# Sliding-window attention with its two heads side by side, and a position bias that a skewed transfer shapes instead of a product

## The chip, the cores and the metric

The kernel runs on one core of one Trainium2 chip. The metric is the device time of one execution in microseconds (us). The engines are named as in the profile: PE (matrix products, with PEld for its weight loads), DVE (vector), ACT (scalar), POOL (GpSimd) and SP (SyncE, which here issues most of the transfers).

## What is computed

Two transformer blocks, sequence 512, width 1024. Only the mixer of the first block is touched by the change. It projects the normed input once, runs sliding-window attention on 8 query heads (2 key heads, 4 queries to a key) and a linear recurrence (rwkv7) on 8 heads, and projects both back.

```
h = rms_norm(x, norm_mix_pre)
proj = h @ w_in                                    # 1024 -> 20 tiles of 128
q, k, v, p = split(proj, (512, 640, 768))
# attention: blocks of 128 queries against their own block and the one before
rel = (arange(128)[:, None] + 128) - arange(256)[None, :]
bias = rel_bias[t5_bucket(rel)]                    # one row of 256 per query: a function of i - j only
scores = q . k * 64**-0.5 + bias ; out of window -> -1e30
m = max(scores.max(-1), sink) ; p = exp(scores - m)
probs = p / (p.sum(-1) + exp(sink - m)) ; attn = probs @ v
# recurrence: 512 steps of state = state*w + sa*(kk*a) + v*k ; o = state . r, per head
mix = concat([attn, rw]) @ w_out
x = x + rms_norm(mix, norm_mix_post)
```

Behind it come a gated feed-forward layer and the second block (two layers with five other kinds of attention and two feed-forward layers), with the same instructions before and after.

## The kernel before

**Dense products.** A unit of a projection is 24 products 128x512 on PE (L237 to L239): 8 slices of the width, each as high x high, low x high and high x low part of weights and activations. Its weights come as one raw transfer of 512 KB by SP, ACT makes the high part (L443), DVE the low part (`wl`, L444). When a unit is done DVE takes its result out of the PSUM bank with the norm's factor (`u`, L638, then the shift L641, or `swq`, L1088). The first projection has 20 units (480 products), the one behind the mixer (`out_first`) 6 slices of 8 units, 144 products.

**The recurrence** is done for four pairs of heads, j = 0 to 3. D_j projects, A_j (`stage_a`) builds small masked products on PE (L734, L735: 64x128, 32 of each) whose results DVE masks out of PSUM (L738 to L740), POOL multiplies decays into operands for it (L700, L704, L706, L717, L718). I_j (`inverse_rows`) inverts triangular 32x32 blocks on DVE: one transpose of 128x1024 (L765), then 62 dependent small operations (L770, L772), and a trip through DRAM on SP's queue. J_j joins the inverse on PE (L797, L807), with DVE's transposes (L792) of what that trip brought back; B_j (`stage_b`) runs the chain over 8 chunks on PE (L837, L856, L869, L871, L882) and DVE (L880).

**The attention** S_j (`swa`) does two heads, one for each key head. It loads the bias (below), then per block of 128 queries makes scores per head (L929, each in a PSUM bank of its own from tag "a"), adds the bias on DVE per head (L930), takes the row maximum (L932), the exponential on ACT (L936), transposes the probabilities on PE (L946), copies them on ACT (L948) and multiplies with the values (L951, output 128 x 64 per head). After four blocks DVE multiplies by 1/l (L966) and PE turns the result (L970).

**The bias.** The table of 8 heads x 384 distances is made once and written to DRAM as 8 rows by POOL's DMA queue (L626, `relscr`). Each S_j reads it by POOL's queue with a row step of one element (L913), which gives the rows in reversed order, and a product with a reversed identity (`J`, L915) puts them right; ACT copies them to `swb` (L917).

**What sets the order.** The program is written stage by stage in the order of CFG's list, `D0 PK A0 D1 Q0 Q1 I0 A1 I1 J0 B0 Q2 S0 Q3 D2 A2 J1 I2 S1 B1 S2 J2 D3 s0 S3 A3 I3 r1 J3 s2 s1 B2 s3 B3 r0 r2 r3 F`, and the framework's scheduler, with buffers' free times by its own estimate of durations, decides when each instruction is placed in its engine's queue. On the chip each queue then runs in that order. `I` stages are raised by a priority of 200.

Of the kernel before, what the change touches and what calls it, by code (L numbers as in the profile page):

```python
# [20 lines left out]
CFG = {'order': 'D0 PK A0 D1 Q0 Q1 I0 A1 I1 J0 B0 Q2 S0 Q3 D2 A2 J1 I2 S1 B1 S2 J2 D3 s0 S3 A3 I3 r1 J3 s2 s1 B2 s3 B3 r0 r2 r3 F', 'inv': 'VVVV', 'rt': 'G', 'bt': 'G', 'bh': 'G', 'kh': 'G', 'kk': 'V', 't1': 'V', 'th': 'G', 'at': 'A', 'ti': 'A', 'sh': 'V', 'bb': 'bbbs', 'ob': 'onno', 'fa': 2, 'oa': 2, 'yc': [1, 1], 'xc': [1, 1], 'xa': ['GVGGGGVV', 'GVGGVGGV'], 'ev': 0, 'mb': 'qqb', 'fb': 'qqb', 'rc': 1, 'xm': [('ld', 'cs', 'th', 'dec')], 'xf': [('z', 'z', 'z', 'z')], 'mp': 'on', 'fp': 'os', 'rkv': 5, 'wo0': 0, 'wo1': 0, 'up': 0, 'wi': 0, 'spare': '', 'ahead': 'bno|a', 'hpi': 200, 'uact': 'A'}  # L21
# [446 lines left out]
def boundary(k, x, h, st, applies, banks, tags, post, more=None):  # L468
# [12 lines left out]
    for i in range(2):  # L481
# [7 lines left out]
      "sws": 2, "swp": 2, "swq": 4, "F": 2, "ST": 3, "s_hw0": 1, "s_om": 1, "s_ha0": 1, "s_hka": 1, "s_pc": 2}  # L489
# [73 lines left out]
def first_mixer(k, I):  # L563
# [24 lines left out]
    hbc = k.rstd(x0, "s", CFG["rc"], CFG["spare"] or None)  # L588
# [26 lines left out]
    def swa_table():  # L615
# [3 lines left out]
        q = k.pstr("a")  # L619
# [13 lines left out]
        SW.update(sink=sk, nsink=nsk, J=J, scr=scr)  # L633
# [274 lines left out]
    def swa(j):  # L908
        kt, vt, qt = SW["k"], SW["v"], SW["q", j]
        rv = k.slot("sws", (P, 2, 256))  # L910
        for g in range(2):
# [27 lines left out]
        def values(b, s):  # L939
            k0 = max(b - 1, 0)  # L940
            nn = b + 1 - k0
            nk = nn * P
            q = k.pstr("a")
# [926 lines left out]
```

## Time and profile before

| | us |
|---|---|
| median of 3 runs | 2228.12 (2227.75 to 2228.48) |
| the profiled execution | 2228.3 |
| its span | 2226.5 |
| PE busy in it | 2147.9 (96%) |
| DVE, ACT, POOL busy | 1387.0 (62%), 920.5 (41%), 350.9 (16%) |

Spans and starts below are counted in the profiled execution from the start of its span; 1.8 us lie around the span. Its mean granted TensorE clock is 0.988 of full speed. The mixer of the first block lies in about the first 350 us. A share of busy time over the whole span says little about these, so the rows further down are cut from them.

### The profile page before, as it was taken

What the parts mean: (1) busy time and instruction counts of PE and PEld (TensorE: products, weight loads), DVE (VectorE), ACT (ScalarE), POOL (GpSimd) and SP (SyncE); (2) the same over time, 40 slices, a digit from 0 to 9 for tenths busy, and PEclk for the clock granted to TensorE, in tenths of its full rate; (3) what the DMA queues carried; (4) which work ended last, traced back from release to release, by engine and by line L of the source; (5) the groups of instructions that cost most, each with busy time, mean ns of one, the idle gap of its engine ahead of it and who ended that gap; (6) DMA issues with size and microseconds to landing.
All of it is one profiled execution on the core that took longest, in us unless ns stands there. A gap on an engine that the chain in (4) does not pass through costs nothing. (4 is left out here: it accounts for less than half of the span.)

```text
span 2226.5 us, 30146 instructions
## 1 busy us (share of the span) xinstructions
PE 2147.9 (96%) x11780; PEld 1718.5 (77%) x11784; DVE 1387.0 (62%) x2494; ACT 920.5 (41%) x1519; POOL 350.9 (16%) x327
## 2 busy tenths in 40 slices
PE   7899997999999999999999999999999899999998
PEld 6677777788888889976667888888666568888887
DVE  4987856766336666544776652664696656644665
ACT  4434534444234444333444442443244444433443
POOL 2111105111001113200101111111013202111111
PEclk9999998999999999999999999999999999999999
DMA  4210130233333235321112333232211012323334
GB/s 158 70 43 26 45 94 30 91 104 100 95 100 99 95 114 174 121 68 48 48 57 80 100 98 100 96 95 95 77 54 61 29 48 87 103 95 95 96 122 152
DMA packets 66302, 192.82 MB, mean 87 GB/s; under 512 B 15808, under 2 KB 19152, under 8 KB 66160
## 3 DMA queue, kind: packets, MB, share of 16 engines
q1 hardware_dynamic: 65584, 189.70, 26.8%
q0 software_dynamic: 576, 1.19, 0.3%
q8 instruction: 93, 1.52, 0.3%
q14 instruction: 49, 0.40, 0.1%
HBM read 188.24 MB, written 2.63 MB: 86 GB/s over the span
## 5 line engine op out<-in xcount | busy, mean ns | idle before, releaser
L444 DVE TENSOR_TENSOR wl<-raw,wh 128x1024 fp32r<-128x1024 f32 x341 | 431.1, 1265 | 261.0 <-ACT wh L443 260.5
L237 PE MATMUL q<-hh,wh 128*128 128x512 f32 (+1 forms) x1294 | 518.2, 401 | 11.1 <-ACT hh L204 8.1
L443 ACT ACTIVATE wh<-raw 128x1024 fp32r<-128x1024 f32 x341 | 359.7, 1056 | 373.9 <-PE q L238 217.1
L238 PE MATMUL q<-hl,wh 128*128 128x512 f32 (+1 forms) x1294 | 506.7, 392 | 5.2 <-DVE hl L205 5.2
L239 PE MATMUL q<-hh,wl 128*128 128x512 f32 (+1 forms) x1294 | 506.0, 391 | 0.0
L237 PEld LDWEIGHTS q<-hh,wh 128*128 128x128 f32 x1294 | 246.3, 190 | 62.5 <-ACT hh L204 8.1
L238 PEld LDWEIGHTS q<-hl,wh 128*128 128x128 f32 x1294 | 246.6, 191 | 54.7 <-DVE hl L205 5.7
L239 PEld LDWEIGHTS q<-hh,wl 128*128 128x128 f32 x1294 | 246.1, 190 | 53.2 <-issue 4.0
L237 PE MATMUL b<-hh,wh 128*128 128x512 f32 (+1 forms) x602 | 237.5, 394 | 0.0
L238 PE MATMUL b<-hl,wh 128*128 128x512 f32 (+1 forms) x602 | 231.6, 385 | 1.5 <-DVE hl L205 1.5
L239 PE MATMUL b<-hh,wl 128*128 128x512 f32 (+1 forms) x602 | 231.8, 385 | 0.0
L288 POOL TENSOR_TENSOR zu<-za,z 128x512 f32<-128x512 f32 x76 | 100.8, 1327 | 814.7 <-DVE z L283 758.6
L237 PE MATMUL q<-gh,wh 128*128 128x256 f32 (+1 forms) x559 | 189.2, 339 | 2.5 <-ACT wh L443 1.4
L239 PE MATMUL q<-gh,wl 128*128 128x256 f32 (+1 forms) x559 | 188.8, 338 | 1.2 <-DVE wl L444 1.1
L238 PE MATMUL q<-gl,wh 128*128 128x256 f32 (+1 forms) x559 | 187.8, 336 | 0.0
L144 ACT ACTIVATE gh<-zu 128x512 fp32r<-128x512 f32 x76 | 48.1, 632 | 250.5 <-POOL zu L288 250.5
L145 DVE TENSOR_TENSOR gl<-zu,gh 128x512 fp32r<-128x512 f32 x76 | 52.6, 692 | 150.8 <-ACT gh L144 150.8
L177 POOL TENSOR_TENSOR nsq<-nsq,nsq 128x256 f32<-128x256 f32 (+1 forms) x84 | 97.1, 1156 | 257.4 <-ACT nsq L172 257.1
L281 ACT ACTIVATE z<-u,pv 128x512 f32<-128x512 f32 x152 | 122.7, 809 | 31.2 <-DVE u L280 31.2
L238 PEld LDWEIGHTS b<-hl,wh 128*128 128x128 f32 x602 | 114.2, 190 | 24.1 <-DVE hl L205 2.4
L239 PEld LDWEIGHTS b<-hh,wl 128*128 128x128 f32 x602 | 114.0, 189 | 23.5 <-issue 1.0
L237 PEld LDWEIGHTS b<-hh,wh 128*128 128x128 f32 x602 | 114.2, 190 | 22.6 <-issue 2.7
(565 smaller groups left out, 3261.4 us busy)
## 6 DMA issues: line engine op xcount, KB each, us to landing
raw<-in_ffn_up SPq DMA_DIRECT2D x88, 512.0 KB, 3.5
raw<-in_w_ffn_up SPq DMA_DIRECT2D x64, 512.0 KB, 3.4
raw<-in_ffn_down SPq DMA_DIRECT2D x55, 512.0 KB, 3.5
raw<-in_w_ffn_down SPq DMA_DIRECT2D x48, 512.0 KB, 3.5
raw<-in_ev_w_in SPq DMA_DIRECT2D x24, 512.0 KB, 3.5
raw<-in_w_in SPq DMA_DIRECT2D x20, 512.0 KB, 3.7
raw<-in_od_w_in SPq DMA_DIRECT2D x20, 512.0 KB, 3.5
x<-in_x SPq DMA_DIRECT2D x16, 256.0 KB, 4.4
```

Of the source, the lines that this page charges most:

```text
L144: nc.scalar.activation(hi, x, AF.Copy)
L145: nc.vector.tensor_tensor(lo, x, hi.bitcast(F32), op=OP.subtract)
L177: (nc.gpsimd if m % chains == 0 else nc.vector).tensor_tensor(acc, acc, sq, op=OP.add)
L237: nc.tensor.matmul(o, wh, xh, start=(k == 0), stop=False)
L238: nc.tensor.matmul(o, wh, xl, start=False, stop=False)
L239: nc.tensor.matmul(o, wl, xh, start=False, stop=(k == n - 1))
L281: nc.scalar.activation(y, v, AF.Identity, bias=col(3), scale=col(2))
L288: nc.gpsimd.tensor_tensor(u, a, z[1], op=OP.mult)
L443: nc.scalar.activation(a, part, AF.Copy)
L444: (nc.gpsimd if self.pool > 0 else nc.vector).tensor_tensor(b, part, a.bitcast(F32), op=OP.subtract)
```

## The change

It edits `first_block` and the PSUM pool. In PSUM the two banks of tag "s" go, their users alternate between the banks "a" and "o", and the two banks form one double tile "w" (`two`) with a single buffer, which the attention, the first norm and the table use. In S_j the scores of both heads go side by side into the two banks of "w" and one DVE operation adds the bias for both. The probabilities of all four blocks are turned first and kept (`pts`), then eight products per j (the two heads alternating between the halves of the output's partitions) give the transposed output at once; 1/l is spread to 128x512 by POOL, turned by PE, copied by ACT and multiplied in by DVE. The bias table is written to DRAM 128 times per head, with rows of 385 of which 384 are filled, so that a read with a row step of 384 from element 127 returns the bias in the right order straight into `swb`; the product with `J`, its constant and ACT's copy go.

```diff
-CFG: 'ob': 'onno'      M1: "swp": 2
+CFG: 'ob': 'nnnw'      M1: "swp": 1
     def pss(self):
-            return self.p1.tile([P, S], F32, name=f"s_{self.ns}", tag="s", bufs=2)
+            return self.bank("ao"[self.ns % 2])
+    def two(self):
+        self.ns += 2
+        return self.p1.tile([P, 2, S], F32, name=f"w_{self.ns}", tag="w", bufs=1)
...
-        scr = k.dr.tile([8, 384], F32, name="relscr")
-        nc.gpsimd.dma_start(scr, vec[:8, :384])
-        J = k.slot("J", (P, P))
-        nc.gpsimd.dma_start(J, I["c_rev"])
+        scr = k.dr.tile([8, P, 385], F32, name="relscr")
+        nc.gpsimd.dma_start(scr[:, :, :384], vec[:8, None, :384].to_broadcast([8, P, 384]))
...
     def swa(j):
-        rv = k.slot("sws", (P, 2, 256))
+        bias = k.slot("swb", (P, 2, 256))
         for g in range(2):
             src = SW["scr"][j + 4 * g]
-            nc.gpsimd.dma_start(rv[:, g], bass.AP(tensor=src.tensor, offset=src.offset, ap=[[1, P], [1, 256]]))
-        q = k.pstr("a")
-        nc.tensor.matmul(q, SW["J"], rv.rearrange("p g k -> p (g k)"), start=True, stop=True)
-        bias = k.slot("swb", (P, 2, 256))
-        nc.scalar.activation(bias, q.rearrange("p (g k) -> p g k", g=2), AF.Copy)
+            nc.gpsimd.dma_start(bias[:, g], bass.AP(tensor=src.tensor, offset=src.offset + 127, ap=[[384, P], [1, 256]]))
...
+            q = k.two()
             for g in range(2):
-                q = k.pstr("a")
-                nc.tensor.matmul(q[:, :nk], qt[gs, b * P:(b + 1) * P], kt[gs, k0 * P:k0 * P + nk], start=True, stop=True)
-                nc.vector.tensor_tensor(s[:, g, :nk], q[:, :nk], bias[:, g, 256 - nk:], op=OP.add)
+                nc.tensor.matmul(q[:, g, :nk], qt[gs, b * P:(b + 1) * P], kt[gs, k0 * P:k0 * P + nk], start=True, stop=True)
+            nc.vector.tensor_tensor(s[:, :, :nk], q[:, :, :nk], bias[:, :, 256 - nk:], op=OP.add)
...
-            for g in range(2):
-                for kb in range(nn):
-                    nc.tensor.matmul(o[:, (2 * b + g) * 64:(2 * b + g + 1) * 64], pT[:, (g * nn + kb) * P:(g * nn + kb + 1) * P],
-                                     vt[:, (k0 + kb) * P + 64 * g:(k0 + kb) * P + 64 * g + 64], start=(kb == 0), stop=(kb == nn - 1))
...
+        wide = k.slot("sws", (P, 8, 64))
+        nc.gpsimd.tensor_copy(wide, ls[:, :, None].to_broadcast([P, 8, 64]))
+        oq = k.two()
+        for kb in range(NB):
+            for g in range(2):
+                n = min(2, NB - kb)
+                nc.tensor.matmul(oq[64 * g:64 * g + 64, 0, kb * P:(kb + n) * P], vt[:, kb * P + 64 * g:kb * P + 64 * g + 64],
+                                 pts[:, g, 2 * kb:2 * kb + n].rearrange("p c t -> p (c t)"), start=(kb == 0), stop=(kb == NB - 1),
+                                 skip_group_check=True)
         for b in range(NB):
-            nc.tensor.transpose(q[:, b * P:(b + 1) * P], tf[:, b * P:(b + 1) * P], k.ident)
-        nc.scalar.activation(qt, q, AF.Copy)
+            nc.tensor.transpose(oq[:, 1, b * P:(b + 1) * P], wide[:, 2 * b:2 * b + 2].rearrange("p a d -> p (a d)"), k.ident)
+        w = k.slot("swp")
+        nc.scalar.activation(w, oq[:, 1], AF.Copy)
+        nc.vector.tensor_tensor(qt, oq[:, 0], w, op=OP.mult)
```

The instructions also stand in another order, in stages that the diff does not edit. The lines of the changed kernel are counted anew: its L738 is L734 of before, L743 to L745 are the dense products, L450 is L444, L642 is L638, L711 is L707, L769 is L765. On PE's queue, before, A0's first masked product is row 235:

```order
L237 MATMUL q_698<-hh_126,wh_701 128x512
L238 MATMUL q_698<-hl_127,wh_701 128x512
L239 MATMUL q_698<-hh_126,wl_702 128x512
L237 MATMUL q_734<-hh_112,wh_737 128x512
L238 MATMUL q_734<-hl_113,wh_737 128x512
L734 MATMUL s_564<-ar_539,ksq_505 64x128
L735 MATMUL s_564<-ar_539,kti_547 64x128
```

After, rows 224 to 449 are dense products but for one pair of scores, and A0's first masked product is row 450:

```order
L244 MATMUL q_2358<-hl_125,wh_2361 128x512
L245 MATMUL q_2358<-hh_124,wl_2362 128x512
L243 MATMUL q_2358<-hh_126,wh_2361 128x512
L244 MATMUL q_2358<-hl_127,wh_2361 128x512
L245 MATMUL q_2358<-hh_126,wl_2362 128x512
L738 MATMUL a_562<-ar_537,ksq_503 64x128
L739 MATMUL a_562<-ar_537,kti_545 64x128
```

So 432 dense products of the first projection stand ahead of A0's first masked product, where 218 stood. The one pair among them is that of S0's first block, both heads in one row of the listing:

```order
L244 MATMUL q_1399<-hl_127,wh_1402 128x512
L245 MATMUL q_1399<-hh_126,wl_1403 128x512
L929 MATMUL w_1439<-swk_446,swq_799 128x128 x2
L243 MATMUL q_1518<-hh_112,wh_1521 128x512
L244 MATMUL q_1518<-hl_113,wh_1521 128x512
```

It stands 121 rows ahead of A0's masked products. On DVE's queue, before, the masks of A0 (L738 to L740) follow ksq (L707) with one `u` and one `wl` between:

```order
L707 TENSOR_TENSOR ksq_505<-ksq_505,ld_492 128x512
L714 TENSOR_TENSOR bon_554<-rkv_445,s_552 128x512
L638 TENSOR_TENSOR u_729<-q_698,bc_352 128x512
L444 TENSOR_TENSOR wl_774<-raw_771,wh_773 128x1024
L738 TENSOR_TENSOR aab_560<-s_564,msk_396 128x2x64
L739 TENSOR_TENSOR aak_561<-s_564,msk_396 128x2x64
L740 TENSOR_TENSOR x_562<-s_564,msk_396 128x2x128
```

After, rows 81 to 100 hold the results of eight units (`u`, `swq`) and ten splits `wl`, and only then come ksq (L711, row 102) and the masks; rows 91 to 102 of them:

```order
L1088 SCALAR_TENSOR_TENSOR swq_1430<-q_1399,bc_352 128x512
L450 TENSOR_TENSOR wl_1555<-raw_1552,wh_1554 128x1024
L1088 SCALAR_TENSOR_TENSOR swq_1549<-q_1518,bc_352 128x512
L450 TENSOR_TENSOR wl_1591<-raw_1588,wh_1590 128x1024
L642 TENSOR_TENSOR u_1582<-q_1551,bc_352 128x512
L450 TENSOR_TENSOR wl_1627<-raw_1624,wh_1626 128x1024
L642 TENSOR_TENSOR u_1618<-q_1587,bc_352 128x512
L450 TENSOR_TENSOR wl_2362<-raw_2359,wh_2361 128x1024
L450 TENSOR_TENSOR wl_2398<-raw_2395,wh_2397 128x1024
L450 TENSOR_TENSOR wl_2434<-raw_2431,wh_2433 128x1024
L645 SCALAR_TENSOR_TENSOR rkv_1584<-u_1582,pv,rkv_1584 128x511
L711 TENSOR_TENSOR ksq_503<-ksq_503,ld_490 128x512
```

I0's transpose is row 97 of DVE before and row 120 after, with 11 and 20 `wl` ahead of it. On POOL's queue, before, the table's write and both reads of S0 stand ahead of A0's first operation (L700):

```order
L626 DMA relscr<-swp_406 8x384
L913 DMA sws_1434<-relscr 128x256 x2
L700 TENSOR_TENSOR ar_539<-rkv_435,dec_501 128x8x64
L704 TENSOR_SCALAR th_499<-th_499 128x512
L706 TENSOR_TENSOR ksq_505<-kk_504,th_499 128x512
L718 TENSOR_TENSOR kk_504<-kti_547,dec_501 128x512
L717 TENSOR_TENSOR th_499<-ksq_505,dec_501 128x512
```

After, the write of 1,024 rows stands ahead of A0's operations and the reads behind four of them:

```order
L632 DMA relscr<-swp_406 1024x1x384
L704 TENSOR_TENSOR ar_537<-rkv_433,dec_499 128x8x64
L708 TENSOR_SCALAR th_497<-th_497 128x512
L710 TENSOR_TENSOR ksq_503<-kk_502,th_497 128x512
L722 TENSOR_TENSOR kk_502<-kti_545,dec_499 128x512
L917 DMA swb_1432<-relscr 128x256 x2
L721 TENSOR_TENSOR th_497<-ksq_503,dec_499 128x512
```

Nothing of A0 is ahead of the write on this queue in either.

## Rows read from the trace of the kernel before

**Rows 1.** Section 1 of the page, the whole execution: busy time of each engine, its share of the span, instructions.

```profile
PE 2147.9 (96%) x11780; PEld 1718.5 (77%) x11784; DVE 1387.0 (62%) x2494; ACT 920.5 (41%) x1519; POOL 350.9 (16%) x327
```

**Rows 2.** Busy time of each engine in stretches of the first 352 us and, for the price of one dense product, in 500 to 800 us. Columns: stretch, its length, busy us and instructions of PE, PEld, DVE, ACT, POOL, granted TensorE clock, busy share of the DMA engines, GB/s.

```profile
66.10:83.10 17.00, 15.29 (x117) 11.73 (x116) 15.63 (x39) 4.98 (x8) 4.42 (x4) 1.00 0.24 84
83.10:275.20 192.10, 185.74 (x1693) 138.39 (x1691) 158.02 (x486) 85.39 (x206) 27.99 (x28) 0.98 0.15 40
275.20:333.00 57.80, 57.56 (x562) 43.46 (x561) 35.02 (x116) 21.13 (x43) 1.47 (x2) 1.00 0.29 87
333.00:352.00 19.00, 14.21 (x79) 11.75 (x77) 10.24 (x28) 6.09 (x11) 4.72 (x6) 0.82 0.15 51
500.00:800.00 300.00, 300.00 (x1326) 248.48 (x1325) 164.81 (x201) 118.81 (x147) 25.89 (x20) 1.00 0.31 98
```

**Rows 3.** Timeline, start and duration in us: the first masked product of A0 on PE (L734), the first mask on DVE (L738), the first transpose of I0 on DVE (L765); then line L765 as a whole (I0 to I3: duration in ns, first and last start in us).

```profile
76.23 0.44 PE L734 MATMUL s<-ar,ksq 64*64 64x128 f32 x4 [0.90 <-DVE ksq L707]
...
79.02 0.28 DVE L738 TENSOR_TENSOR aab<-s,msk 128x128 f32<-128x128 f32 x1
...
83.05 2.00 DVE L765 STREAM_TRANSPOSE invm<-aab 128x1024 f32<-128x1024 f32 x1 [0.38 <-ACT aab L764]
...
L765 DVE STREAM_TRANSPOSE invm<-aab x4: 1952/1972/2002, 83.1 to 275.2; 128x1024 f32<-128x1024 f32 x4
```

**Rows 4.** Waits of PE from I0's transpose to I3's (83.1 to 275.2 us): what waited for what, us in total, times, longest; the first and the last of five.

```profile
PE s L693 <- DVE kti L690: 3.3, 1, 3.3
...
PE a L929 <- ACT swb L917: 0.2, 1, 0.2
```

**Rows 5.** Waits of DVE in the same stretch. Of the list's 15 rows the eight left out come to between 0.3 and 1.1 us each.

```profile
DVE sws L930 <- PE a L929: 7.1, 18, 1.2
DVE u L638 <- PE q L239: 5.7, 4, 2.2
DVE swp L966 <- PE o L951: 3.4, 3, 2.2
DVE aab L738 <- PE s L735: 3.2, 4, 2.0
DVE ST L880 <- PE b L871: 2.4, 8, 0.5
DVE invm L765 <- ACT aab L764: 1.8, 3, 0.8
...
DVE swq L1088 <- PE q L239: 0.3, 1, 0.3
```

**Rows 6.** DVE by line and shape in the same stretch: count, busy us, mean ns of one, idle time before them.

```profile
L444 DVE TENSOR_TENSOR wl<-raw,wh 128x1024 fp32r<-128x1024 f32 x11 | 13.4, 1220 | 0.6 <-ACT wh L443 0.6
L930 DVE TENSOR_TENSOR sws<-a,swb 128x256 f32<-128x256 f32 x24 | 10.1, 419 | 6.1 <-PE a L929 6.0
...
L641 DVE SCALAR_TENSOR_TENSOR rkv<-u,pv,rkv 128x511 f32<-128x511 f32 x7 | 6.0, 863 | 0.1
...
L638 DVE TENSOR_TENSOR u<-q,bc 128x512 f32<-128x512 f32 x7 | 4.8, 689 | 5.7 <-PE q L239 5.7
...
L1088 DVE SCALAR_TENSOR_TENSOR swq<-q,bc 128x512 f32<-128x512 f32 x4 | 2.7, 686 | 0.3 <-PE q L239 0.3
...
L930 DVE TENSOR_TENSOR sws<-a,swb 128x128 f32<-128x128 f32 x8 | 2.2, 281 | 1.2 <-PE a L929 1.1
```

**Rows 7.** Timeline of PE at the attention's products: the bias product (L915), the products with the values (L951, eight records) and one head's scores over 256 keys (L929, two records); then, from the second block, the scores of two heads that lie on the two row halves (L1102, four records) and sixteen products with values that lie on the two column halves (L1140, two each of 512, 384, 256 and 128 columns for either head); last, line L929 as a whole.

```profile
108.13 1.02 PE L915 MATMUL a<-sws,J 128*128 128x512 f32 x2
112.44 1.08 PE L693 MATMUL s<-ident,kti 128*128 128x128 f32 x4 [3.29 <-DVE kti L690]
...
261.53 1.10 PE L951 MATMUL o<-swv,swp 128*128 128x64 f32 x8
262.56 0.70 PE L929 MATMUL a<-swk,swq 64*128 64x256 f32 x2
...
1045.93 2.37 PE L1140 MATMUL o<-PT,avt 128*64 128x512 f32 x16
...
1049.13 0.70 PE L1102 MATMUL s<-ak,aq 64*128 64x256 f32 x4
...
L929 PE MATMUL a<-swk,swq x64: 272/376/579, 115.2 to 264.7; 64*128 64x256 f32 x48, 64*128 64x128 f32 x16
```

**Rows 8.** Timeline of POOL from the write of the bias table (L626) to A0's first operation, with the idle time before each; then two rows of the DMA issues (KB each, us from issue to landing).

```profile
54.91 0.52 POOL L626 DMA_DIRECT2D relscr<-swp  x1 [23.54 <-DVE swp L624]
58.56 1.12 POOL L913 DMA_DIRECT2D sws<-relscr  x2 [3.13 <-PE q L239]
63.10 2.42 POOL L700 TENSOR_TENSOR ar<-rkv,dec 128x512 f32<-128x512 f32 x1 [3.42 <-ACT dec L678]
...
raw<-in_w_in SPq DMA_DIRECT2D x20, 512.0 KB, 3.7
...
relscr<-swp POOLq DMA_DIRECT2D x1, 12.0 KB, 3.1
```

**Rows 9.** The windows view once more, at a stretch right behind PE's longest wait of [rows 4] (columns as in rows 2).

```profile
112.00:119.00 7.00, 6.56 (x17) 4.24 (x18) 6.69 (x11) 0.94 (x2) 3.45 (x3) 0.55 0.50 111
```

More of the change, by code (lines that the diff above doesn't have):

```diff
@@ L19 @@
 DRAM = bass.MemoryType.DRAM
-CFG = {'order': 'D0 PK A0 D1 Q0 Q1 I0 A1 I1 J0 B0 Q2 S0 Q3 D2 A2 J1 I2 S1 B1 S2 J2 D3 s0 S3 A3 I3 r1 J3 s2 s1 B2 s3 B3 r0 r2 r3 F', 'inv': 'VVVV', 'rt': 'G', 'bt': 'G', 'bh': 'G', 'kh': 'G', 'kk': 'V', 't1': 'V', 'th': 'G', 'at': 'A', 'ti': 'A', 'sh': 'V', 'bb': 'bbbs', 'ob': 'onno', 'fa': 2, 'oa': 2, 'yc': [1, 1], 'xc': [1, 1], 'xa': ['GVGGGGVV', 'GVGGVGGV'], 'ev': 0, 'mb': 'qqb', 'fb': 'qqb', 'rc': 1, 'xm': [('ld', 'cs', 'th', 'dec')], 'xf': [('z', 'z', 'z', 'z')], 'mp': 'on', 'fp': 'os', 'rkv': 5, 'wo0': 0, 'wo1': 0, 'up': 0, 'wi': 0, 'spare': '', 'ahead': 'bno|a', 'hpi': 200, 'uact': 'A'}
+CFG = {'order': 'D0 PK A0 D1 Q0 Q1 I0 A1 I1 J0 B0 Q2 S0 Q3 D2 A2 J1 I2 S1 B1 S2 J2 D3 s0 S3 A3 I3 r1 J3 s2 s1 B2 s3 B3 r0 r2 r3 F', 'inv': 'VVVV', 'rt': 'G', 'bt': 'G', 'bh': 'G', 'kh': 'G', 'kk': 'V', 't1': 'V', 'th': 'G', 'at': 'A', 'ti': 'A', 'sh': 'V', 'bb': 'bbbs', 'ob': 'nnnw', 'fa': 2, 'oa': 2, 'yc': [1, 1], 'xc': [1, 1], 'xa': ['GVGGGGVV', 'GVGGVGGV'], 'ev': 0, 'mb': 'qqb', 'fb': 'qqb', 'rc': 1, 'xm': [('ld', 'cs', 'th', 'dec')], 'xf': [('z', 'z', 'z', 'z')], 'mp': 'on', 'fp': 'os', 'rkv': 5, 'wo0': 0, 'wo1': 0, 'up': 0, 'wi': 0, 'spare': '', 'ahead': 'bno|a', 'hpi': 200, 'uact': 'A'}
 P = 128
@@ L99, in bank @@
             return self.pss()
+        if tag == "w":
+            return self.two()[:, 0]
         if PAIRS == 2 and tag in "ab":
@@ L488 @@
 M1 = {"u": 2, "rkv": 5, "bon": 2, "aab": 2, "vt": 2, "bht": 2, "kht": 2, "ar": 2, "RT": 1, "rq": 2, "rwo": 2,
-      "sws": 2, "swp": 2, "swq": 4, "F": 2, "ST": 3, "s_hw0": 1, "s_om": 1, "s_ha0": 1, "s_hka": 1, "s_pc": 2}
+      "sws": 2, "swp": 1, "swq": 4, "F": 2, "ST": 3, "s_hw0": 1, "s_om": 1, "s_ha0": 1, "s_hka": 1, "s_pc": 2}
 def first_block(k, I, ctx):
@@ L587, in first_mixer @@
     nc.sync.dma_start(k.pv[:, PV["cw1"]:], I["pv"][:, PV["cw1"]:])
-    hbc = k.rstd(x0, "s", CFG["rc"], CFG["spare"] or None)
+    hbc = k.rstd(x0, "w", CFG["rc"], CFG["spare"] or None)
     k.ahead(st, h, 0, banks=list((CFG["ahead"] + "|").split("|")[1]))
@@ L609, in swa_proj @@
         v = evac(k, k.proj(st, h), "u", hbc)
-        SW["v"] = k.to_rows(v, "swv", "a")
+        SW["v"] = k.to_rows(v, "swv", "w")
     def swa_q(j):
@@ L618, in swa_table @@
         nc.gpsimd.dma_start(rb[:32], I["rel_bias"])
-        q = k.pstr("a")
+        q = k.pstr("w")
         nc.tensor.matmul(q[:8, :384], rb[:32, :8], oh[:32, :384], start=True, stop=True)
@@ L632, in swa_table @@
         nc.vector.tensor_scalar(nsk, sk, -1.0, None, op0=OP.mult)
-        SW.update(sink=sk, nsink=nsk, J=J, scr=scr)
+        SW.update(sink=sk, nsink=nsk, scr=scr)
     def shifted(i, name):
@@ L937, in probs, with turned @@
             return s
[L939 to L943, printed above, removed]
+        def turned(b, s):
+            nn = b + 1 - max(b - 1, 0)
+            q = k.pstr("w")
             for g in range(2):
@@ L946, in values @@
                     nc.tensor.transpose(q[:, (g * nn + kb) * P:(g * nn + kb + 1) * P], s[:, g, kb * P:(kb + 1) * P], k.ident)
-            pT = k.slot("swp")
-            nc.scalar.activation(pT[:, :2 * nk], q[:, :2 * nk], AF.Copy)
-            for g in range(2):
-                for kb in range(nn):
-                    nc.tensor.matmul(o[:, (2 * b + g) * 64:(2 * b + g + 1) * 64], pT[:, (g * nn + kb) * P:(g * nn + kb + 1) * P],
-                                     vt[:, (k0 + kb) * P + 64 * g:(k0 + kb) * P + 64 * g + 64], start=(kb == 0), stop=(kb == nn - 1))
+            nc.scalar.activation(pts[:, :, max(2 * b - 1, 0):2 * b + 1], q[:, :2 * nn * P].rearrange("p (g c t) -> p g c t", g=2, t=P), AF.Copy)
         prev = probs(0)
@@ L958, in swa @@
                 prev = probs(b + 1)
-            values(b, cur)
+            turned(b, cur)
         nc.vector.tensor_tensor(es.rearrange("p (b g) -> p b g", g=2), es.rearrange("p (b g) -> p b g", g=2),
```

8 lines of the change are left out of this document (1 added, 7 removed).

## The prediction

> **What bounds the kernel now.** PE is busy for 96% of the span [rows 1]. That is an average, so I cut the first 352 us, where all that the change touches lies, into stretches at the inversions I0 and I3, whose transposes are easy to find: they start at 83.1 and 275.2 us [rows 3]. Between them PE is busy for 185.7 of 192.1 us and DVE for 158.0; in the next 58 us PE never rests [rows 2]. PE's own waits there are single ones, the longest 3.3 us [rows 4]. DVE's 15 rows of waits add up to 29.2 us, nearly all of them for PE [rows 5]. So PE is the bound and DVE runs beside it with about 15% of slack. What feeds this balance is the order: the recurrence starts at 76.2 us [rows 3], when less than half of the first projection is done, and the other half of its dense products fills PE whenever the chain I, J, B keeps it waiting. Two questions decide: how much work the change takes from PE and DVE, and whether that overlap stays.
>
> **PE's work.** Each of these is a row's duration, whose modelled end makes it a little long.
> - The bias product goes: four of 1.02 us [rows 7], 4.1.
> - Scores: one head over 256 keys takes 0.70 us as two records; in the second block four records on the two row halves, two heads' worth, take 0.70 too [rows 7]. So a pair side by side costs what one head costs. Of 64 records 48 are of 256 columns [rows 7], twelve pairs; with the four of 128 columns at about half, all pairs together would save 12 x 0.70 = 8.4 and about 1.8. Three of the 16 pairs are split by other products in the new order, and I take 7.
> - Values: eight records of 64 columns take 1.10, so the 112 take 15.4. The new products have two records each too and cover 1,792 columns per j for both heads and both records; the second block's sixteen on column halves cover 2,560 in 2.37 us [rows 7], which makes 1.66 per j, 6.6 in all: 8.8 saved. If they ran one after the other only, twice that, and 2.2 saved.
> - The turning of probabilities and of the last tile stays in number (in the first the output, now 1/l).
>
> The sum is about 20 us, between 6 (nothing runs together) and 22. ACT loses four copies and gains as many, POOL gains four copies of 128x512 at about 1 to 2.4 us each (as its other operations) and is idle most of the time [rows 2, 8]: nothing.
>
> **The table.** POOL's write of 8 rows takes 0.52 us to issue and lands in 3.1; a read of 128 rows takes 0.56 to issue [rows 8]. For 1,024 rows I have no row. From below it is 0.5 us; from above, eight reads' worth, 4.5. A0's first operation on POOL starts at 63.1 after 3.4 us of idle, and the read that stood ahead of it started at 58.6 [rows 8], so even the upper end delays A0 by a few us at most. The 1.57 MB are three raw weight loads of 512 KB at 3.7 us [rows 8], 11 us of transfer if nothing shares them. They run beside weight loads with the DMA engines 24% busy [rows 2], and SP loads up to three raws ahead, that is 3 x 24 products at 0.226 = 16 us of PE's work. I take nothing; uncovered it is up to 11.
>
> **The order, which outweighs all that.** In the new order 432 dense products stand ahead of A0's first masked product on PE, where 218 stood. A dense product costs 300.0/1326 = 0.226 us [rows 2]. PE executes in this order, so that product, at 76.2 before [rows 3], comes 214 x 0.226 = 48.4 us later, and with the first block's scores at about 125. Nothing makes it earlier: no product of this recurrence stands higher. Before, I0's transpose followed 6.8 us behind it (76.23 to 83.05) with one `wl` between (1.22 in the mean [rows 6]) [rows 3]; in the new order that `wl` is ahead and one or two adds of S0 come between, so I take 5.5: **I0's transpose at 130.5**, 47.4 late. DVE has little to do in these 48 us: ten splits and eight results, and then waits for PE.
>
> From there DVE has everything still to do that is not a split or a result of the projection. Between I0's and I3's transposes it needed 192.1 - 29.2 = 162.9 us besides its waits [rows 3, 5]. What leaves this stretch:
> - nine `wl` splits (20 instead of 11 ahead of I0) of 1.22 [rows 6]: 11.0;
> - four `u` of 0.69, two shifts of 0.86 and four `swq` of 0.69 [rows 6]: 7.3;
> - the adds: 12.3 in 32 operations [rows 6] become sixteen, twelve of 512 elements at the 0.69 of another operation from PSUM of that size [rows 6] and four at 0.42, 10.0 in all, of which 1.1 is ahead of I0: 3.4 saved.
>
> The final multiply stays. So DVE needs 162.9 - 21.7 = 141.2 us and can't finish I3's entry before 130.5 + 141.2 = 271.7 even if it never waits. PE now has less to do there: 203 of 258 dense products are gone from the stretch, 45.9 us, and the 20 of above, 185.7 - 45.9 - 20 = 120 us. **DVE becomes the bound** of this stretch, and PE stands about a quarter of the time.
>
> DVE's waits after are the open term. From 29.2 [rows 5] I take the 5.7 and 0.3 for results of dense units, which are now ahead, and half of the 7.1 at the adds, of which there are half as many; I add 2 (a choice, no row prices it) at J's entry, where with less filler ahead the trip of the inverse through DRAM isn't covered any more: 21.6. The lower bound is 5 (the masks' and the transposes' own, 3.2 + 1.8), the upper 35: waits for PE's chain, which dense products lengthened, may shorten, but two engines in fixed order that wait for each other may also wait more. This gives 130.5 + 141.2 + 21.6 = 293.3 for I3's transpose against 275.2: **18.1 us late**.
>
> Behind I3 both orders hold the same: the chain I3, J3, B3 with the dense products of `out_first` as filler, 53 to 54 us of PE's work to the last product of B3 in either, since s and r stages and the 144 products stay there. I take 0, and up to 4 for a filler that runs out elsewhere. The sum: 2228.3 (this execution, 0.2 over the runs' median) + 18.1 = 2246.4.
>
> **The clock** is a second open term. At 112 to 119 us, right behind PE's 3.3 us of idleness, the granted clock is 0.55, near the lower level of 1.2 GHz [rows 4, 9]; at 333 to 352, where PE is 75% busy, its mean is 0.82 [rows 2]. The new stretch has PE at about 120 of 163 us, like the latter. At 0.82 PE's 120 us become 146, still under DVE's 163, so by these rows the sum stands. The Trainium skill, "TensorE: Matmul & The Clock Gate", section "A second HAM failure mode: psum-queue depth-cycling", has a kernel whose PE idled briefly between groups of products and whose clock swung between the two levels with loss of throughput; by that rule this change pays beside the order for what it does to the clock. The trace agrees that the clock falls behind idleness; what many short waits do no stretch of it shows.
>
> **The rivals.**
> - *Faster: the thinner attention pays.* PE was the bound and loses 20 us; kept in balance the time would be 2228.3 - 20 = 2208. For it: 185.7 of 192.1 [rows 2]. Against it: the late start of A0. With that start, the best is DVE without waits, 271.7 instead of 275.2, 3.5 us gained, 2225; it decides where DVE's waits fall under 3.5 us in total, or where A0's products come more than 20 us sooner than counted.
> - *About the same: DVE's waits shrink* to 5 to 10, since PE, no longer loaded with dense work, answers at once. For it: most rows of [rows 5] are waits for PE. Then 1.5 to 6.5 us late, 2230 to 2235.
> - *Much slower: the clock.* If PE runs at half in most of the stretch, its 120 us become up to 240, more than DVE's 163, and every answer to DVE takes twice: DVE's waits at 43 instead of 21.6 give 2268, PE as bound more. For it [rows 9]; against it the 0.82 of [rows 2].
> - *The table's write* holds POOL or the weight loads for far longer than I bound: 11 us on top, 2257. The Trainium skill, "DMA: Bandwidth & Descriptors", section "Issuing engines are not separate DMA queues", says that transfers of all issuing engines run on the same DMA engines and interleave; no run here shows what the write does to the loads.
> - *It doesn't do what it says*: pairs of scores and of value products run one after the other. Then PE saves 6 instead of 20 and has 134 us in the stretch, still hidden: 2246 to 2250.
>
> **How the numbers follow.** The forecast and the pairs that don't pair together, 0.62, give 2246, with a range of their own of 2236 to 2260 (waits of 11 to 35). Waits of 10 or less 0.13, half of it within 0.2%, which is 4.5 us and about what a measurement of this kernel can tell. Clock 0.12, write 0.05, faster 0.08. So slower 0.62 + 0.06 + 0.12 + 0.05 = 0.85, same 0.07, faster 0.08. The range leaves out the faster case and the worst half of the clock's: 2228 to 2268.
>
> **What would show it.** In the changed kernel's trace: I0's first transpose at about 130 and its last at about 293; PE without a break from 66 to 124 us on dense products, DVE idle for about half of 85 to 124; from 130 to 293 PE at about 75% and DVE at 87%; pairs of scores at 0.70; the write's issue under 5 us. Wrong would be a transpose of I0 before 110 us, or DVE's waits in the stretch under 10 or over 40.

## The result, and the profile after

The changed kernel takes 2260.5 us (median of 4, 2258.4 to 2262.8) beside 2227.9: 1.0147 of the time before, interval 1.0130 to 1.0165, or 33 us slower. The forecast was 2246, slower, in a range of 2228 to 2268.

Lines of the page of the changed kernel: busy time, PE in 40 slices and the granted clock in tenths.

```profile
PE 2155.3 (95%) x11724; PEld 1719.7 (76%) x11728; DVE 1386.8 (61%) x2478; ACT 919.0 (41%) x1515; POOL 355.4 (16%) x330
...
PE   8988889899999999999999999999999899999998
...
PEclk9988789999999999999999999999999999999999
```

PE's busy time does not fall below that of [rows 1], as one would hope from a thinner attention; it rises by 7 us, and the clock dips in the third to sixth slice. The two markers of [rows 3], the transpose that opens I0 to I3 (now L769) and the first masked product of A0 (now L738):

```profile
L769 DVE STREAM_TRANSPOSE invm<-aab x4: 1912/1928/1984, 142.4 to 308.4; 128x1024 f32<-128x1024 f32 x4
L738 PE MATMUL a<-ar,ksq x64: 269/417/472, 131.5 to 304.4; 64*64 64x128 f32 x64
```

I0 opens at 142.4 us where it was 83.1, so 59 us late, and I3 at 308.4 where it was 275.2, 33 us late. Behind it nothing changes: 2259.1 - 308.4 = 1950.7 us to the end of the span, before 2226.5 - 275.2 = 1951.3. So 59 us are lost before I0, 26 of them are won back between I0 and I3, and 33 stay. Stretches of the changed kernel, columns as in [rows 2]:

```profile
60.00:70.00 10.00, 9.45 (x41) 6.90 (x40) 9.08 (x23) 2.93 (x4) 2.31 (x2) 1.00 0.61 86
70.00:80.00 10.00, 7.10 (x32) 5.54 (x30) 3.29 (x5) 0.52 (x1) 2.65 (x2) 0.97 0.56 104
80.00:90.00 10.00, 9.37 (x29) 7.02 (x30) 5.07 (x6) 3.96 (x6) 1.14 (x2) 0.68 0.66 189
90.00:100.00 10.00, 10.00 (x45) 8.04 (x43) 3.14 (x3) 1.59 (x3) 0.00 (x0) 1.00 0.35 115
...
120.00:131.40 11.40, 7.95 (x36) 6.24 (x34) 3.78 (x5) 2.73 (x3) 0.00 (x0) 0.97 0.32 98
131.40:142.40 11.00, 10.87 (x74) 8.05 (x75) 5.14 (x17) 3.03 (x8) 1.05 (x1) 0.50 0.11 42
142.40:308.40 166.00, 138.50 (x1304) 97.80 (x1303) 135.71 (x446) 70.61 (x180) 31.04 (x31) 0.80 0.07 17
308.40:366.00 57.60, 56.15 (x655) 42.85 (x654) 33.52 (x111) 18.82 (x43) 2.42 (x3) 1.00 0.26 76
```

The reader is to see four things. From 90 us PE runs through the dense products that now stand ahead. In 70 to 90 there is a hole that I had not expected (PE 7.10 of 10 busy, then a clock of 0.68). When A0's products come at last, the clock is at 0.50, the lower of its two levels, and they take 11 us. Between I0 and I3 PE is busy for 138.5 of 166.0 us, 83%, at a clock of 0.80, and DVE for 135.7.

The hole goes with the table's write. Here is the write on POOL, in ns, with its time from issue to landing in us; then the same time of the raw weight loads issued between 50 and 90 us, in the kernel before and in the changed one; then waits of ACT (50 to 142 us) and of PE (8 to 132 us).

```profile
L632 POOL DMA_DIRECT2D relscr<-swp x1: 1100/1100/1100, 50.3 to 50.3; - x1
DMA to landing us min/median/max: 34.8/34.8/34.8
```

```profile
DMA to landing us min/median/max: 3.4/3.5/4.0
DMA to landing us min/median/max: 3.3/18.5/21.9
```

```profile
ACT wh L449 <- DMA raw<-in_w_in: 15.8, 2, 12.3
...
PE a L738 <- DVE ksq L711: 3.5, 1, 3.5
PE q L243 <- ACT wh L449: 3.5, 1, 3.5
```

The write takes 1.1 us to issue and 34.8 us to land, and beside it the raw weight loads take 18.5 us in the median where they took 3.5: ACT waits 12.3 us for one of them, PE in turn for ACT, and the DMA engines are 56 to 66% busy where they were 24% [rows 2]. That the write is the cause is shown by e7, which has the late order and a fast write in its place.

### The profile page after: what moved, and what is told of

Its sections match the earlier page's. It is cut to its first block, busy times and chain, and to the rows that moved or that the text cites. A ratio compares the mean times of both kernels' runs of the same rounds, so it can differ in the third digit from the quotient of the medians.

```text
span 2259.1 us, 30036 instructions
## 1 busy us (share of the span) xinstructions
PE 2155.3 (95%) x11724; PEld 1719.7 (76%) x11728; DVE 1386.8 (61%) x2478; ACT 919.0 (41%) x1515; POOL 355.4 (16%) x330
## 5 line engine op out<-in xcount | busy, mean ns | idle before, releaser
L450 DVE TENSOR_TENSOR wl<-raw,wh 128x1024 fp32r<-128x1024 f32 x341 | 430.7, 1263 | 280.6 <-ACT wh L449 280.0
```

Of the source, the lines that this page charges most:

```text
L450: (nc.gpsimd if self.pool > 0 else nc.vector).tensor_tensor(b, part, a.bitcast(F32), op=OP.subtract)
```

## The experiments

Each is compared with the kernel before on the same chip. The table gives the starts of I0's and I3's transpose, the time between, and the rest of the span, all from one profile of each; the ratio is that of the timed runs, with its interval.

| kernel | I0 | I3 | between | rest | ratio to before |
|---|---|---|---|---|---|
| before | 83.1 | 275.2 | 192.1 | 1951.3 | 1 |
| after | 142.4 | 308.4 | 166.0 | 1950.7 | 1.0147 [1.0130, 1.0165] |
| e1 attention only | 81.4 | 273.1 | 191.7 | 1949.4 | 0.9991 [0.9981, 1.0002] |
| e2 table only | 136.5 | 317.5 | 181.0 | 1957.6 | 1.0253 [1.0218, 1.0288] |
| e3 write by SP | 81.2 | 282.9 | 201.7 | 1948.8 | 1.0043 [1.0029, 1.0057] |
| e4 late, no wide write | 147.8 | 309.5 | 161.7 | 1953.1 | 1.0189 [1.0169, 1.0209] |
| e5 table copied in DRAM | 79.8 | 269.0 | 189.2 | 1950.2 | 0.9956 [0.9938, 0.9974] |
| e6 write by ACT | 99.2 | 280.3 | 181.1 | 1949.3 | 1.0009 [0.9997, 1.0020] |
| e7 late order alone | 128.8 | 298.4 | 169.6 | 1947.9 | 1.0099 [1.0077, 1.0120] |
| e8 e5, splits to POOL | 79.7 | 267.5 | 187.8 | 1948.3 | 0.9964 [0.9950, 0.9977] |
| e9 e5's table, old attention | 81.1 | 270.9 | 189.8 | 1951.7 | 0.9988 [0.9980, 0.9997] |
| e10 e5, less DVE | 80.5 | 259.5 | 179.0 | 1951.5 | 0.9946 [0.9932, 0.9960] |
| e11 e5, less PE | 78.8 | 263.5 | 184.7 | 1950.9 | 0.9953 [0.9937, 0.9970] |

**Which half of the change costs: e1 and e2.** e1 is the changed kernel with the table of before:

```diff
-        scr = k.dr.tile([8, P, 385], F32, name="relscr")
-        nc.gpsimd.dma_start(scr[:, :, :384], vec[:8, None, :384].to_broadcast([8, P, 384]))
+        scr = k.dr.tile([8, 384], F32, name="relscr")
+        nc.gpsimd.dma_start(scr, vec[:8, :384])
 (and in swa: the read with a step of one, the product with J, the ACT copy)
```

> The changed kernel with the bias table as before (8 rows written, read reversed, product with J, ACT copy); the attention stays as changed. Its order has 219 dense products ahead of A0's first masked product, as before (218). Theory: the loss lies in the table's wide write, through the order and the transfer. Then the side by side scores and the new value products show their saving on a PE that is the bound: about 16 us less what the double bank makes wait, 2228 - 14 = 2214, 2208 to 2224, and I0's transpose at 81 to 86. Rival: the attention's single double bank is what costs; then 2240 or more, with waits for w.

Measured: 0.9991 [0.9981, 1.0002], 2223.4 us beside 2225.0. The order of before is back and the loss is gone, so the attention does not cost. But the 14 us of gain did not come either: the interval allows 4 us at most. Its stretch from I0 to I3, columns as in [rows 2]:

```profile
81.40:273.10 191.70, 177.34 (x1651) 128.95 (x1650) 157.04 (x469) 87.07 (x206) 31.36 (x32) 0.96 0.15 40
```

PE is busy for 8.4 us less than in [rows 2], DVE for 157.0 instead of 158.0, and the stretch is as long as before, 191.7.

e2 is the mirror: the kernel before with only the table part of the change.

```diff
-        scr = k.dr.tile([8, 384], F32, name="relscr")
-        nc.gpsimd.dma_start(scr, vec[:8, :384])
-        (J and its product, ACT copy)
+        scr = k.dr.tile([8, P, 385], F32, name="relscr")
+        nc.gpsimd.dma_start(scr[:, :, :384], vec[:8, None, :384].to_broadcast([8, P, 384]))
```

> The kernel before with only the wide table, its skewed reads and no product with J. 432 dense products stand ahead of A0's first masked product. Theory: as slow as the changed kernel or a few us more, since DVE keeps its 32 adds: 2258 to 2270, the write landing after some 35 us, I0's transpose at 135 to 145. Rival (the attention costs): 2224, the four products and copies saved.

Measured: 1.0253 [1.0218, 1.0288], slower than the whole change and past the expected 2270. The stretch from I0 to I3 and the three largest waits of DVE in it (L923 is the scores' product, L924 the add, L945 the products with the values):

```profile
136.50:317.50 181.00, 153.33 (x1325) 112.46 (x1326) 131.98 (x454) 67.72 (x177) 27.79 (x27) 0.77 0.07 16
DVE sws L924 <- PE a L923: 12.7, 10, 3.6
DVE ST L878 <- PE b L869: 11.1, 8, 1.9
DVE swp L960 <- PE o L945: 6.7, 3, 4.2
```

So the table part makes the whole loss. With A0 late and the old attention, DVE waits for 44.8 us in this stretch where it waits for 26.4 in the changed kernel (12.7 against 4.4 of them at the adds), and the stretch is 15 us longer than the changed kernel's 166.0, though DVE is busy for less. By the ratios the new attention, which brings almost nothing in the old order, earns some 1.06% here. The rest behind I3 is 7 us longer as well, with the clock at 0.85 in its first 22 us; why stays open.

**Order or transfer: e3, e4, e6.** e3 gives the wide write to SP:

```diff
-        nc.gpsimd.dma_start(scr[:, :, :384], vec[:8, None, :384].to_broadcast([8, P, 384]))
+        nc.sync.dma_start(scr[:, :, :384], vec[:8, None, :384].to_broadcast([8, P, 384]))
```

> The changed kernel with the wide write on SP's queue instead of POOL's; 219 dense products ahead of A0's first masked product. Theory that the order is most of it and the transfer the rest: I0's transpose at 83 to 95 and 2212 to 2228, by how much the 35 us of transfer hold the weights back. Rival that the transfer is nearly all: 2245 to 2260 though the order is back.

Measured: 1.0043 [1.0029, 1.0057], 2233.5 us, between the two. I0 is early (81.2), as the theory has it, but the stretch behind it is 10 us longer than before. SP's queue shows why; a stretch of the windows, and SP's wait at the inverse's trip through DRAM (us in all, times, longest):

```profile
85.00:115.00 30.00, 16.67 (x105) 11.64 (x103) 27.86 (x97) 5.67 (x11) 6.75 (x5) 0.63 0.02 4
SPq L778 <- DVE invt L776: 67.3, 3, 60.6
```

The fillers, the dense products that keep PE at work while it waits for I0, need weights whose loads stand on SP behind the DMAs of the inverse (L778), and these wait for I0 to be done: seven loads of the projection that stood ahead of them in the kernel before now come after. In this stretch 11 dense products run where the kernel before has 83, and PE is 16.67 of 30 us busy, at a clock of 0.63. The move put right one order and broke another, so it does not separate the transfer's share.

e4 makes the order late without the wide write, on e1, by the list of stages:

```diff
-'D0 PK A0 D1 Q0 Q1 I0 A1 I1 J0 B0 Q2 S0 Q3 D2 A2 J1 I2 S1 B1 S2 J2 D3 s0 S3 ...
+'D0 PK D1 Q0 Q1 Q2 Q3 D2 D3 A0 I0 A1 I1 J0 B0 S0 A2 J1 I2 S1 B1 S2 J2 s0 S3 ...
```

> The first of these four with the stages A0 and I0 set behind all projections in the list of stages: 432 dense products ahead of A0's first masked product as in the changed kernel, but 8 rows written. Order alone: I0's transpose at 128 to 132 and 2244 to 2250 (my sum of 18 us, and the products with J). If the transfer alone made the loss: 2214, as the first.

Measured: 1.0189 [1.0169, 1.0209], 2266.1 us; a miss, 16 us over the top of what was expected. I0 opens at 147.8. The stretches before it:

```profile
110.00:120.00 10.00, 6.73 (x26) 3.56 (x24) 6.18 (x17) 2.46 (x3) 1.12 (x1) 0.83 0.30 102
120.00:130.00 10.00, 7.56 (x28) 5.99 (x28) 3.10 (x8) 1.06 (x1) 1.09 (x1) 0.82 0.01 2
130.00:140.00 10.00, 7.56 (x42) 6.10 (x43) 5.73 (x12) 1.35 (x2) 3.99 (x3) 0.52 0.16 52
```

The list moved not only A0's masked products but all of A0 behind the projections, so its chain of lora product, norm and decays, which hides under dense products in both kernels, lay bare from 112 to 147 us. That is not the changed kernel's order, and e4 says only that a late recurrence costs.

e6 gives the wide write to ACT:

```diff
-        nc.gpsimd.dma_start(scr[:, :, :384], ...)
+        nc.scalar.dma_start(scr[:, :, :384], ...)
```

> The changed kernel with the wide write from 8 partitions issued by ACT. 243 dense products ahead of A0's first masked product, so the order is nearly that of before while the slow write still runs beside the weight loads, and SP's queue holds nothing new. If the transfer costs by itself: 10 us over e5 (raw loads landing late, PE waiting for wh), 2228 to 2240. If it only cost through the order: as e5 within 4 us.

Measured: 1.0009 [0.9997, 1.0020], 2231.9 us, 11 us over e5, as expected but not by the cause that I named. POOL's timeline, with its idle time ahead of the first row:

```profile
85.04 1.09 POOL L917 DMA_DIRECT2D swb<-relscr  x2 [56.54 <-DMA relscr<-swp]
86.16 0.63 POOL L708 TENSOR_SCALAR th<-th 128x512 f32<-128x512 f32 x1
```

POOL, idle for 56.5 us, stands until 85.0 at S0's reads of the table, which the order puts ahead of A0's operations and which wait for the landing of the write issued at 50.6; A0's products then wait 9.3 us for DVE, which waits for POOL. The raw loads beside this write land late too (15.1 us in the median between 50 and 90 us), but no wait of ACT or PE for them shows. So this is a wait in POOL's queue, and the price of the transfer beside the weight loads is not isolated by it.

**The write made fast: e5 and e7.** e5 keeps the whole change but makes the wide table in two steps, with 128 as the outer dimension:

```diff
-        nc.gpsimd.dma_start(scr[:, :, :384], vec[:8, None, :384].to_broadcast([8, P, 384]))
+        scr0 = k.dr.tile([8, 384], F32, name="relrow")
+        nc.gpsimd.dma_start(scr0, vec[:8, :384])
+        nc.gpsimd.dma_start(scr[:, :, :384].rearrange("h p k -> p h k"),
+                            bass.AP(tensor=scr0.tensor, offset=scr0.offset, ap=[[0, P], [384, 8], [1, 384]]))
```

> The changed kernel with the wide table made in two steps: 8 rows written as before, then copied inside DRAM to 128 times 8 rows. 219 dense products ahead of A0's first masked product. Theory: the slow landing comes from a source of 8 partitions; the copy lands in under 15 us, I0's transpose is at 81 to 86, and the time is that of e1 less what the products with J cost, 2217 to 2226. Rival (the 1.57 MB hold the weights however they are written): 2235 or more.

Measured: 0.9956 [0.9938, 0.9974], 2220.6 beside 2228.5 us. It beats both kernels. I0 opens at 79.8. The copy on POOL and its landing:

```profile
L634 POOL DMA_DIRECT2D relscr<-relrow x1: 1052/1052/1052, 52.2 to 52.2; - x1
DMA to landing us min/median/max: 10.8/10.8/10.8
```

The same 1.57 MB, from DRAM with 128 outermost, land in 10.8 us instead of 34.8. The Trainium skill, "DMA: Bandwidth & Descriptors", section "Rules for kernel authors", says that the slowest dimension of the access patterns sets how many DMA engines share a transfer and that an outermost dimension below 16 confines it to at most that many. The slow write has its 8 partitions outermost, and these two landings agree with that rule; the runs do not separate it from the change of the source's place, since one reads SBUF and the other DRAM.

e7 is e5 with A0's preparation left where it is and its masked products set behind D3:

```diff
+        yield                                  # in stage_a, ahead of the masked products
         aab, aak = k.slot("aab", (P, 8, C)), k.slot("aak", (P, 8, C))
-'D0 PK A0 D1 Q0 Q1 I0 A1 I1 J0 B0 Q2 S0 Q3 D2 A2 J1 I2 S1 B1 S2 J2 D3 s0 S3 ...
+'D0 PK A0 D1 Q0 Q1 Q2 D2 D3 +0 I0 A1 I1 J0 B0 Q3 S0 A2 J1 I2 S1 B1 S2 J2 s0 S3 ...
 (and in the loop over the list: A0 runs up to the yield, +0 runs the rest of it)
```

> As e5, with the masked products of A0 moved behind D3 in the list of stages while their preparation stays: 432 dense products ahead of A0's first masked product, A0's preparation early, 20 splits ahead of I0, as in the changed kernel, without its slow write. By my sum for the order alone I0's transpose is at 128 to 133 and the time 2240 to 2252. If the order does it all: 2258 to 2264. If the write did most of it: 2230.

Measured: 1.0099 [1.0077, 1.0120], which is 22 us over before by the ratio (the median of 2252.3 stands beside 2228.5) and 2248.1 in the profiled execution. The transposes, A0's first masked product, and the stretch between I0 and I3:

```profile
L773 DVE STREAM_TRANSPOSE invm<-aab x4: 1934/1954/1997, 128.8 to 298.4; 128x1024 f32<-128x1024 f32 x4
L742 PE MATMUL a<-ar,ksq x64: 269/320/473, 122.5 to 294.9; 64*64 64x128 f32 x64
128.80:298.40 169.60, 144.51 (x1315) 101.61 (x1316) 135.44 (x449) 72.07 (x187) 30.25 (x31) 0.78 0.07 17
```

With the late order and the fast table I0 opens at 128.8 and the time rises by 22 us. The rest of the changed kernel's 33, 0.48% or 11 us (about 5 to 17 by the two intervals), goes with the slow write: I0 at 142.4 instead of 128.8. The hole shows it too; e7 from 70 to 90 us, and its raw loads issued between 50 and 90:

```profile
70.00:90.00 20.00, 19.07 (x86) 15.89 (x87) 12.47 (x17) 5.40 (x7) 4.97 (x3) 1.00 0.34 106
DMA to landing us min/median/max: 3.4/3.6/6.4
```

With as many dense products ahead, and 1.57 MB written as well, PE is busy for 19.07 of these 20 us at full clock, where the changed kernel has 16.47 at 0.83; the raw loads land in 3.6 us instead of 18.5, and ACT has no wait for one. So the slow write, not the order and not its bytes alone, holds the loads back.

**What sets the pace in the old order: e8 to e11.** e1 had shown that 8 to 16 us less on PE bring 4 us at most, so I tried DVE. e8 lets POOL make four splits:

```diff
-            (nc.gpsimd if self.pool > 0 else nc.vector).tensor_tensor(b, part, ...)
+            (nc.gpsimd if self.pool > 0 or self.nu in self.on else nc.vector).tensor_tensor(b, part, ...)
 (with on = (12, 14, 16, 18) for the first projection alone)
```

> e5 with the low parts wl of four weight units behind I0 (12, 14, 16 and 18 of the first projection) made by POOL instead of DVE: 5 us of DVE's work gone from the stretch between I0 and I3, PE's work unchanged. If DVE and its waits set the pace of that stretch in the early order: 4 to 6 us under e5, 2214 to 2217. If PE sets it, as I read in the kernel before: as e5 within 2 us. If POOL's slower operation comes too late for PE: over e5.

Measured: 0.9964 [0.9950, 0.9977], as e5. It decides nothing, for DVE's work did not shrink. First e5's stretch from I0 to I3, then e8's; and in the same order two lines of DVE, an operation on 8 columns in A and the token shift:

```profile
79.80:269.00 189.20, 179.13 (x1677) 131.59 (x1675) 157.31 (x475) 85.35 (x207) 32.59 (x32) 0.94 0.15 43
```

```profile
79.70:267.50 187.80, 173.55 (x1652) 129.46 (x1651) 158.47 (x467) 84.24 (x202) 41.40 (x36) 0.95 0.15 42
```

```profile
L706 DVE TENSOR_SCALAR ar<-kk 128x8 f32<-128x8 f32 x3 | 0.5, 162 | 0.0
...
L648 DVE SCALAR_TENSOR_TENSOR rkv<-u,pv,rkv 128x511 f32<-128x511 f32 x7 | 6.1, 873 | 0.1
```

```profile
L708 DVE TENSOR_SCALAR ar<-kk 128x8 f32<-128x8 f32 x3 | 3.7, 1240 | 0.0
...
L650 DVE SCALAR_TENSOR_TENSOR rkv<-u,pv,rkv 128x511 f32<-128x511 f32 x7 | 8.1, 1161 | 1.6 <-ACT rkv L649 1.6
```

Four splits are gone, but DVE is busy for 158.5 instead of 157.3 us: with POOL at 41 instead of 33 us the three operations on 8 columns take 3.7 us instead of 0.5 and the seven shifts 1.16 us each instead of 0.87 (other lines, not shown, move both ways). That POOL's work does this is possible, but it was not tried apart; the dependent additions of the inverse, for one, went from 208 to 231 ns here and stand at 225 and 226 in e11 and e1, which have no split on POOL.

e10 takes the four splits off DVE without giving them to POOL, and e11 takes products off PE:

```diff
e10
+            if self.nu in self.on:                        # units 12, 14, 16, 18
+                nc.scalar.activation(b, part, AF.Copy)    # instead of the subtraction on DVE
e11
-                nc.tensor.matmul(o, wh, xl, start=False, stop=False)
+                if not (isinstance(w, Stream) and w.nu - 1 in w.on):
+                    nc.tensor.matmul(o, wh, xl, start=False, stop=False)
```

> e5 with the low parts wl of the same four weight units written by ACT as a plain copy (so the values of these four units are not the reference's): four operations of 1.29 us, 5.1 us, gone from DVE between I0 and I3, nothing added to POOL, PE's work as in e5. If DVE and its waits set the pace there: 4 to 6 us under e5, at about 2215. If PE sets it: as e5 within 2 us.

> e5 without the second of the three products per slice (high part of the weights by low part of the activations) in four weight units between I0 and I3, so that their values are not the reference's: 32 dense products, 7.2 us, gone from PE, DVE's work as in e5. If PE sets the pace: 6 to 8 us under e5, at about 2213. If DVE and its waits set it: as e5 within 2 us.

Measured: e10 0.9946 [0.9932, 0.9960], e11 0.9953 [0.9937, 0.9970]. Both intervals overlap e5's, so by the times neither is shown to be under e5. The full 7.2 us, which PE as the only bound would give, lie outside what the intervals of e11 and e5 allow (about 6 at most, the two taken together); the 5.1 us of DVE lie within. The stretch in the one profile of e10 and of e11 (e5's stands above), and then 170 to 200 us in e5 and in e10:

```profile
80.50:259.50 179.00, 166.80 (x1654) 124.69 (x1653) 152.38 (x467) 87.35 (x207) 31.51 (x32) 0.99 0.15 44
78.80:263.50 184.70, 173.31 (x1632) 126.69 (x1631) 155.41 (x474) 85.15 (x207) 30.07 (x32) 0.93 0.15 44
```

```profile
170.00:200.00 30.00, 28.55 (x283) 20.93 (x278) 24.41 (x65) 13.24 (x36) 8.41 (x8) 0.72 0.10 28
170.00:200.00 30.00, 26.69 (x361) 20.07 (x360) 26.72 (x80) 16.94 (x49) 9.00 (x9) 1.00 0.09 29
```

Against e5's 189.2 both are shorter, e10 by more than its own work, e11 by less. But e5's profile has a piece at a clock of 0.72 where e10's is at 1.00, so part of e10's ten us may be the clock and not DVE's work, and one profile does not tell whether such a dip belongs to the kernel or to that execution. So PE alone is not the bound in the old order; how much belongs to DVE and its waits stays open.

e9 is the kernel before with e5's table and without J, its attention untouched (the edit is that of e5, on before).

> The kernel before with the wide table copied inside DRAM, its skewed reads and no product with J; its attention as before; 218 dense products ahead of A0's first masked product. PE loses four products of 1.02 us and ACT four copies. If PE sets the pace: 4 us under before, 2222 to 2226, and e5 a further 16 under it (which e5 does not show). If the stretch is set by DVE and its waits: within 3 us of before, e5 4 to 8 under it.

Measured: 0.9988 [0.9980, 0.9997], 2.5 us under before by the medians. By the ratios e9 is 2.7 us under before (0.7 to 4.5) and e5 9.8 (5.8 to 13.8). So the table without J is worth 2 to 3 and the attention, on top of it, some 7 (about 3 to 12), of the 16 us of PE's work that I had counted for it. On the old table the same attention gained 2 us (e1, none to 4); whether the two halves help each other or only the intervals hide the sum stays open.

## Why the prediction was right, and where its terms were off

- **The whole: right in direction, with luck in the number.** The time came out slower for the reason given. But 2260.5 lies 14 us over the forecast and just past the 2236 to 2260 of its own case, and the wider range that holds it had been stretched for the clock, not for what happened.
- **A0 late through the order: right.** The start of I0 by order alone was forecast at 130.5; e7, which has that order and no slow write, opens it at 128.8, and its time is 22 us over before where the sum had 18.
- **The table's write, "I take nothing": wrong.** This is the term that was mis-sized. I bounded the issue (0.5 to 4.5 us; 1.1 measured) and took the transfer at the rate of the weight loads, 11 us, hidden by three raws ahead. It took 34.8, three times the bound; that I used a row of 128 partitions for a source of 8 is the likely reason, though e5 changed the source's place as well. The loads fell behind (18.5 us in the median), A0's first product came at 131.5 instead of 125 (122.5 in e7), and behind PE's 3.5 us of waiting it met the lower clock, so that it was 11.0 instead of 5.5 us to I0. That is 12 of the 14 us between forecast and result; e7 against after gives 11. It was a rival (11 us on top, 2257, at a chance of 0.05) with a mechanism of the right kind, and came on top of the likeliest case.
- **DVE's stretch: nearly right.** 162.8 forecast, 166.0 measured: 139.6 besides DVE's waits, with the gaps between its instructions, and 26.4 of waits (forecast 141.2 and 21.6). DVE is busy for 82% of it and PE for 83%, where I had said 87 and about 75: PE's 138.5 us at a clock of 0.80 stand against 120 at the full clock, or 146 at 0.82. That DVE's own work sets the pace here was not tested by taking work off either engine; in e2 DVE has less work and more waits, and the stretch is longer, so the waits for PE count as much. The largest waits are not those of [rows 5]:

```profile
DVE ST L884 <- PE b L875: 6.5, 8, 1.5
DVE sws L930 <- PE w L929: 4.4, 6, 1.4
DVE aab L742 <- PE a L739: 4.1, 3, 2.1
DVE kk L698 <- PE a L697: 3.5, 2, 2.5
```

The waits at the adds did fall, from 7.1 to 4.4, and those for dense results vanished; waits at the state's chain (L884) grew from 2.4 to 6.5 and those at the masks from 3.2 to 4.1, on a PE at a clock of 0.80, where I had expected 0.82 from [rows 2]. The trip through DRAM that I added 2 us for shows no wait.
- **Pairs side by side: right.** Two rows of PE's timeline in the changed kernel, four records of scores of 256 keys, which is both heads, and ten of the sixteen records of the new products with the values:

```profile
184.52 0.70 PE L929 MATMUL w<-swk,swq 64*128 64x256 f32 x4 [1.40 <-DVE sws L930]
...
211.33 1.30 PE L964 MATMUL w<-swt,swv 128*64 128x256 f32 x10
```

Four records take 0.70 us, as one head did in [rows 7], and ten of 256 columns 1.30. At the lower clock they take longer: four such records of scores at 189.6 us, in a stretch at 0.50, took 1.23. (By my own rows the most that PE could save was 23 us, 4.1 and 10.2 and 8.8, not 22; nothing rests on it.)
- **"PE is the bound" before: too simple.** The faster rival rested on it (2208 if PE's 20 us counted in full). e1 has the old order and a PE 8 us less busy, and gains nothing that its interval tells; e5 gains 10, and e11, by its interval and e5's, leaves no room for all of PE's work to count. So the 97% of [rows 2] is no proof of a bound. A likely reason is that the fillers on PE spread into whatever room the chain of DVE leaves. From before to e1 to e5 the granted clock in the stretch falls from 0.98 to 0.96 to 0.94, so that in these profiles part of the work saved comes back as slower work; it is no rule, for e10, whose PE is busy for 93% of its stretch, has 0.99.

## What to carry to other kernels

When a scheduler places instructions by its own durations, look first at where the edited stage's neighbours went: here one write on POOL's queue moved a stage that the diff does not touch by 214 products, and that cost 22 us where the better products and the table earn 10 (e5). On SP's queue, or as a copy inside DRAM, the same bytes left the stage in place; that the scheduler reckons the slow write long is likely and not shown. Price a transfer by a row with the same kind of source and the same outermost dimension, not by its bytes. An engine that is busy for 97% of a stretch with work that can stand anywhere is not yet its bound: take a few us off it and see whether the stretch gets shorter.

## What the runs showed of the hardware

- 1.57 MB written from 8 partitions landed after 34.8 to 35.0 us (after, e2); the same bytes copied inside DRAM with 128 outermost after 10.6 to 11.4 (e5, e7 to e11).
- Raw weight loads of 512 KB issued beside the slow write landed after 18.5 us in the median (after; 13.2 in e2, 15.1 in e6), where they took 3.5 in the kernel before and 3.6, at most 6.4, with the copy in its place (e7; all issued between 50 and 90 us).
- With four splits of 128x1024 on POOL (2.4 us each, e8) DVE's seven shifts took 1.16 us each, where they took 0.74 to 0.97 in before, e1, e5, e9, e10 and e11; the cause was not tried apart.
- A0's masked products of 64x128, on a clock of 0.50 from 131 to 142 us, take 417 ns in the median in the changed kernel, and 270 in the kernel before at a clock of 1.00; between 90 us and the first of them PE had rested once, for 3.5 us.
